# Up projections of latent attention moved beside the merge-logit pairs, block sums formed earlier, raw latents parked in DRAM

## The chip, the cores and the metric

The kernel runs on one core of one Trainium2 chip. The metric is device time of one execution in microseconds (us). Five engines work beside each other, each with its own instruction queue that is worked off in order: TensorE (PE, matmuls, with its weight loads PEld), VectorE (DVE), ScalarE (ACT), GpSimd (POOL, here mostly an issuer of DMAs) and SyncE (SP, issues DMAs). All PE results land in PSUM banks, from which ACT and DVE take them.

## The reference, cut to what matters

Two layers, each on a stream of 1024 tokens and 1024 channels:

```python
def hybrid_layer(x, c_act, cos, sin, ...):
    u = x * (1.0 + scale[:, None, :]) + shift[:, None, :]
    proj = jnp.einsum("bsd,dp->bsp", u, w_in)
    a_in, a_gate, b_in, b_gate, q_lat, kv_lat, k_rope, c_gate, merge_logits = jnp.split(proj, split_pts, axis=-1)
    ...                     # A: GLU, causal conv of 31 taps, LayerNorm, swish; B: conv of 3 taps, gated
    q = jnp.einsum("bsr,rk->bsk", rms_norm(q_lat, q_norm_g), w_uq).reshape(b, s, MLA_HEADS, QK_NOPE + QK_ROPE)
    kv = jnp.einsum("bsr,rk->bsk", rms_norm(kv_lat, kv_norm_g), w_ukv).reshape(b, s, MLA_HEADS, QK_NOPE + V_HEAD)
    ...                     # rotary parts, causal attention of 8 heads, times SiLU(c_gate)
    m = g_a * y_a + g_b * y_b + g_c * y_c          # g = sigmoid(merge_logits)
    out = jnp.einsum("bsd,de->bse", m, w_o)
    return layer_norm(DEEPNORM_ALPHA * x + gate[:, None, :] * out, ln_g, ln_b)
```

## The kernel before, in words

Everything is channel-major: a tile is 128 channels by 512 tokens, and the tokens are two halves, h = 0 and 1. Each float32 operand is split into a rounded high part and the rest (`split`, lines 124 to 133: a copy on ACT, L129, then a subtraction on DVE, L130), and each product is three matmuls (high by high, high by low, low by high). So every weight block of 128x512 costs an ACT and a DVE instruction before PE can use it.

A layer is a list of jobs in the order in which they are to run; `run` issues them one after the other and loads the weights of jobs up to four units ahead. The program is then ordered within each engine's queue by a scheduler, so that an instruction may move a little from the place of its job. `weave` and `blend` merge two lists, by number of jobs and by stated cost of PE work.

- **The head of a layer.** For each half the two kv and three q latents are products of u with W_in (`latps`, L186 to L188, four jobs of six matmuls each) and the rotary key (`krps`). Each raw latent is copied to a tile `lat` of the tag `w` (six buffers of 128x512 for the whole kernel), and its squares are summed. `rstd_jobs` makes the RMS factor from that (a sum over channels on PE, `qv`, then eight short DVE instructions `rs` and a row that PE spreads, `rstd`). `norm` scales the raw latents and splits them into pairs `latn`.
- **The up projections** (`up_jobs`): `kps` (k without rotation), `vps` (values), `qps`, and `x1ps` with `x2ps` (rotary q). Each result is split into a tile of the tag `sp` (two buffers) and stored to DRAM by a DMA on POOL's queue.
- **The block sums** (`s_job`, four of them): from the four x tiles of a channel pair (two channel blocks by two token halves) it makes the sums S1 to S4. Four x tiles (`xu`, tag `w`) are loaded on SP's queue and scaled on ACT, and four subtractions or additions and four splits follow on DVE and ACT.
- **The pairs** (`pair_jobs`): two channel blocks of a projection by all 1024 tokens are made with seven block products instead of eight (Strassen's scheme in Winograd's form), from X11, S1, S2, X12, S3, S4, X22. A pair is 84 matmuls at L295. The sums for all channels must be there before its second product is done. Twelve pairs make the merge logits (`lgps`), then come A (`aps`), C's gate (`cgps`), B (`xgps`, `bgps`) and A's gate (`agps`). The 31-tap convolution of each A pair is 31 DVE instructions on 128x1024 (L721, L725), woven beside the logit pairs that follow (`fill`).

Before the change one layer runs: the head of h = 0 with the u tiles (layer 1: the LayerNorm of the layer before) beside it; then `mix`, the head of h = 1 blended with the up projections of h = 0, with the four `s_job`s put in at four places; then two logit pairs blended with the up projections of h = 1; then four times an A pair and three further pairs with its convolution; then the B pairs with the LayerNorm of A (`lna`), and A's gates.

Of the kernel before, what the change touches and what calls it, by code (L numbers as in the profile page):

```python
# [16 lines left out]
P = 128  # L17
T = 512
# [28 lines left out]
def homes(a, b):  # L47
# [7 lines left out]
    "kvn0": ["u23", "u22"], "qn0": ["u11", "u7", "u19"], "kvn1": ["ab", "ab"], "qn1": ["c0", "c1", "c2"],  # L55
# [45 lines left out]
class Trunk:  # L101
# [391 lines left out]
    def s_job(self, l, i):  # L493

        nc = self.nc
        x11, x12, x21, x22 = (self.affine(l, h, 2 * i + e, act=True) for h in range(2) for e in range(2))
        tt = nc.vector.tensor_tensor
        tt(x11, x11, x21, op=ALU.subtract)
        self.factor(l, "S3", x11)
        tt(x21, x21, x22, op=ALU.add)  # L500
        self.factor(l, "S1", x21)
        tt(x22, x22, x11, op=ALU.subtract)
        self.factor(l, "S2", x22)
        tt(x12, x12, x22, op=ALU.subtract)
        self.factor(l, "S4", x12)
# [41 lines left out]
    def rms_jobs(self, l, h, which, tags=None):  # L547
        nc = self.nc
        st = {"t": []}
        n, ch, g = (3, CH_Q, V_QG) if which == "q" else (2, CH_KV, V_KG)  # L550

        def chunk(j):
            def fn(ps):
# [8 lines left out]
                st["t"].append(t)  # L562
            return self.in_chunk(l, h, ch + j, fn, "latps", tags[j] if tags else "pj")

        def norm(_):
            r = st["r"]
            res = []
            for j, t in enumerate(st["t"]):
                v = self.vec[l][:, g + j:g + j + 1]
                nc.vector.scalar_tensor_tensor(t[:, :T], t[:, :T], v, r, op0=ALU.mult, op1=ALU.mult)  # L570
                p = self.pair(f"{which}n{h}", "latn")
                self.split(p, t[:, :T])
                res.append(p)
            self.state[which + "n", l, h] = res
        return [chunk(j) for j in range(n)], self.rstd_jobs(st, 128 * n, "rms", ("tp", "tp")) + [([], norm)]
# [578 lines left out]
    def head(self, l, h, tags=(None, None)):  # L1154
# [3 lines left out]
        lat = kv[0] + kv[1] + weave(q[0] + q[1] + q[2], kvn, 2, 10) + self.krope_job(l, h)  # L1158
        ukv, uq = self.up_jobs(l, h)
        return lat, weave(ukv, qn, 0, 3) + uq  # L1160
# [15 lines left out]
    def build(self):  # L1176
        self.setup_early()
        jobs, first, adas = [], [], []
        for l in range(L):
# [29 lines left out]
            lat1, up1 = self.head(l, 1)  # L1209
            sums = [([], lambda _, l=l, i=i: self.s_job(l, i)) for i in range(4)]  # L1210
            n = len(up0)
            mix = blend(lat1, up0)
            where = [i for i, j in enumerate(mix) if any(j is u for u in up0)]
            for at, sj in sorted(zip((6, 12, where[4], where[-1]), sums), key=lambda p: -p[0]):
                mix.insert(at + 1, sj)
            jobs += mix

            lg = [self.logit_pair(l, n, 2 * i) for n in range(3) for i in range(4)]
            body = blend(lg[0] + lg[1], up1)
            convs = [self.conv_jobs(l, j) for j in range(4)]  # L1220
            fill = [lg[2] + lg[3] + lg[4], lg[5] + lg[6] + lg[7], lg[8] + lg[9] + lg[10],
# [156 lines left out]
```

## Time and profile before

| | before |
|---|---|
| median of 3 runs | 2282.19 us (2275.01 to 2285.17) |
| profiled execution, its own time | 2280.31 us |
| its span in the profile | 2278.1 us |
| busy: PE, DVE, ACT, POOL | 94%, 80%, 50%, 10% of the span |
| mean granted TensorE clock | 0.976 of full speed |

The busy share is an average over stages. PE is nearly always busy from the A pairs on, and has its holes in the heads of the two layers and around the attention. A matmul that runs at the lower clock counts as busy too, for longer.

### The profile page before, as it was taken

Reading aid. Unit: us, or ns where it says so; the run is one execution under the profiler, and the core shown is the slowest. Engines: PE = TensorE matmul, PEld = TensorE weight load, DVE = VectorE, ACT = ScalarE, POOL = GpSimd, SP = SyncE. Lnnn points to the kernel's source line nnn. Section 1 sums busy time; section 2 is a strip of 40 time slices with the busy share of each in tenths; the row PEclk is TensorE's granted clock in tenths of the full one; section 3 lists DMA queues with packets and bytes.
Section 4 is the critical chain, followed back from the end, with each engine's and each line's share of the span. In section 5 each row is a group of like instructions: output and inputs, shape, how many; then the busy total and the mean of one; then the engine's idle time right before and its main releaser. Section 6 shows DMA issues by size and latency. Waiting matters only on the chain.

```text
span 2278.1 us, 29704 instructions
## 1 busy us (share of the span) xinstructions
PE 2148.4 (94%) x10097; PEld 1724.4 (76%) x10097; DVE 1815.8 (80%) x2910; ACT 1139.8 (50%) x2072; POOL 226.4 (10%) x467
## 2 busy tenths in 40 slices
PE   8788999999999999988997799999999999999896
PEld 7566888888778778866775578888887778888686
DVE  4677789989887678777867868889898867867786
ACT  2665333333443656656447553334334447666753
POOL 4001000000001321101001010000000023211000
PEclk9989999999999999998999899999999999999998
DMA  7467322223222996665537572222222259755442
GB/s 262 151 202 225 120 105 105 101 100 108 77 82 89 231 243 183 183 178 184 187 108 208 188 216 82 90 102 93 84 92 70 65 155 226 207 135 149 156 158 65
DMA packets 181606, 328.28 MB, mean 144 GB/s; under 512 B 22096, under 2 KB 46928, under 8 KB 181456
## 3 DMA queue, kind: packets, MB, share of 16 engines
q1 hardware_dynamic: 122256, 214.30, 30.1%
q0 software_dynamic: 45376, 86.93, 14.8%
q10 hardware_dynamic: 13824, 25.17, 2.9%
q8 instruction: 79, 1.29, 0.2%
q14 instruction: 71, 0.58, 0.1%
HBM read 249.96 MB, written 76.35 MB: 143 GB/s over the span
## 4 chain that ended last, share of the span: by engine, by line
PE 78%; issue 9%; DMA 5%; DVE 5%; ACT 3%; POOL 0%; SPq 0%; POOLq 0%; DVEq 0%; ACTq 0%
PE lgps L295 21%; PE bgps L295 7%; PE xgps L295 7%; PE aps L295 7%; PE cgps L295 3%; PE yps L186 3%; PE agps L295 3%; PE yps L187 3%; PE yps L188 3%; PE avps L943 3%; PE tps L927 3%; PE ops L186 2%; PE ops L187 2%; PE ops L188 2%; PE score L903 1%
## 5 line engine op out<-in xcount | busy, mean ns | idle before, releaser
L295 PE MATMUL lgps<-u,wsplit 128*128 128x512 f32 x2016 | 477.4, 395 | 2.0 <-ACT u L129 0.8
L129 ACT CAST wsplit<-wraw 128x512 fp32r<-128x512 f32 (+1 forms) x524 | 318.4, 615 | 304.9 <-DVE wraw L220 45.6
L295 PEld LDWEIGHTS lgps<-u,wsplit 128*128 128x128 f32 x2016 | 377.3, 188 | 96.3 <-ACT u L129 1.8
L130 DVE TENSOR_TENSOR wsplit<-wraw,wsplit 128x512 fp32r<-128x512 f32 (+1 forms) x524 | 354.3, 681 | 69.8 <-ACT wsplit L129 67.8
L725 DVE SCALAR_TENSOR_TENSOR cacc<-abuf,vec,cacc 128x1024 f32<-128x1024 f32 x240 | 307.4, 1281 | 0.5
L295 PE MATMUL bgps<-u,wsplit 128*128 128x512 f32 x672 | 160.5, 397 | 0.0
L295 PE MATMUL xgps<-u,wsplit 128*128 128x512 f32 x672 | 159.9, 397 | 0.0
L295 PE MATMUL aps<-u,wsplit 128*128 128x512 f32 x672 | 158.3, 395 | 0.0
L295 PEld LDWEIGHTS xgps<-u,wsplit 128*128 128x128 f32 x672 | 126.3, 188 | 31.3 <-issue 1.0
L295 PEld LDWEIGHTS bgps<-u,wsplit 128*128 128x128 f32 x672 | 125.8, 188 | 31.7 <-issue 1.8
L295 PEld LDWEIGHTS aps<-u,wsplit 128*128 128x128 f32 x672 | 126.0, 188 | 30.8
L130 DVE TENSOR_TENSOR pt<-tps,pt 128x512 fp32r<-128x512 f32 (+1 forms) x160 | 100.9, 634 | 35.5 <-ACT pt L129 34.3
L129 ACT CAST pt<-tps 128x512 fp32r<-128x512 f32 (+1 forms) x160 | 85.7, 540 | 74.2 <-PE tps L927 71.4
L943 PE MATMUL avps<-pt,Vh 128*128 128x256 f32 x640 | 120.0, 302 | 2.3 <-ACT pt L129 2.0
L908 DVE TENSOR_REDUCE nm<-score 128x1 f32<-128x384 f32 (+7 forms) x128 | 95.8, 751 | 28.4 <-PE score L906 27.8
L186 PE MATMUL yps<-y,wsplit 128*128 128x512 f32 x256 | 107.0, 421 | 9.8 <-DVE mf L1014 5.9
L910 ACT ACTIVATE prob<-score,nm 128x384 f32<-128x384 f32 (+7 forms) x128 | 94.3, 740 | 43.2 <-PE tps L927 25.0
L186 PE MATMUL ops<-m,wsplit 128*128 128x512 f32 (+1 forms) x320 | 115.3, 360 | 0.0
L188 PE MATMUL ops<-m,wsplit 128*128 128x512 f32 (+1 forms) x320 | 113.1, 353 | 0.0
L187 PE MATMUL ops<-m,wsplit 128*128 128x512 f32 (+1 forms) x320 | 112.9, 353 | 0.0
L927 PE MATMUL tps<-cs,prob 128*128 128x128 f32 x576 | 92.6, 278 | 15.6 <-DVE pt L130 15.2
L943 PEld LDWEIGHTS avps<-pt,Vh 128*128 128x128 f32 x640 | 95.2, 194 | 14.5 <-ACT pt L129 7.8
(316 smaller groups left out, 4262.6 us busy)
## 6 DMA issues: line engine op xcount, KB each, us to landing
wraw<-in_win SPq DMA_DIRECT2D x264, 256.0 KB, 2.6
wraw<-in_wout SPq DMA_DIRECT2D x96, 256.0 KB, 3.0
mt<-tD SPq DMA_DIRECT2D x96, 256.0 KB, 4.4
adaraw<-in_wada SPq DMA_DIRECT2D x64, 256.0 KB, 3.3
wraw<-in_wo SPq DMA_DIRECT2D x64, 256.0 KB, 3.1
tD<-mt ACTq DMA_DIRECT2D x48, 256.0 KB, 2.0
Kh<-knD POOLq DMA_DIRECT2D x48, 256.0 KB, 5.0
Vh<-vD POOLq DMA_DIRECT2D x48, 256.0 KB, 5.2
```

The lines of the kernel that those rows point to most:

```text
L129: nc.scalar.copy(dst[:, 0], src)
L130: nc.vector.tensor_tensor(dst[:, 1], src, dst[:, 0].bitcast(F32), op=ALU.subtract)
L186: mm(ps, w[:, 0, c], x[k][:, 0, cols], start=k == 0, stop=False)
L187: mm(ps, w[:, 0, c], x[k][:, 1, cols], start=False, stop=False)
L188: mm(ps, w[:, 1, c], x[k][:, 0, cols], start=False, stop=k == n - 1)
L295: mm(ps, w[:, a, c], x[:, e], start=n < 2 and k == 0 and i == 0, stop=k == 3 and i == 2, skip_group_check=True)
L725: nc.vector.scalar_tensor_tensor(acc, a[:, k:k + S], w, acc, op0=ALU.mult, op1=ALU.add)
L903: mm(o, q[0:96, 0, qc], k[0:96, 0, :w], start=True, stop=False)
L908: nc.vector.tensor_reduce(nm[:, 0:1], sp[:, :nk], axis=AX.X, op=ALU.max, negate=True)
L910: nc.scalar.activation(p[:, :nk], sp[:, :nk], AF.Exp, bias=nm[:, 0:1], accum_out=nm[:, 1:2])
L927: nc.tensor.transpose(tp[:, c:c + P], st["p", hd, 2 * half + b][:, (2 * kp + k) * P:(2 * kp + k + 1) * P], self.ident)
L943: mm(av[:, half * 256:(half + 1) * 256], v[:, 2 * kp + k], pt[:, w, (1 - k) * 256:(2 - k) * 256], start=kp == 0 and k == 0 and w == 0, sto ...
```

## The change

The jobs are put in another order, and some get another home for their tiles; what is computed stays the same. Of the raw latents only the kv latents of h = 0 stay in their `w` tiles. The other eight of a layer are written to DRAM tensors `latq...` and `latkv...` on POOL's queue and read back on SP's queue when `norm` wants them, which is now one job per latent. The `mix` stage holds only the head of h = 1 and the four block sums. The up projections of h = 0 stand beside three logit pairs, those of h = 1 beside the next three, together with the first convolution. The first B pair moves into the last `fill`. `s_job` loads its third and fourth x tile later.

```diff
-    "kvn0": ["u23", "u22"], "qn0": ["u11", "u7", "u19"], "kvn1": ["ab", "ab"], "qn1": ["c0", "c1", "c2"],
+    "kvn0": ["ab", "ab"], "qn0": ["c0", "c1", "c2"], "kvn1": ["c3", "ab"], "qn1": ["c1", "c2", "c3"],
...
     def s_job(self, l, i):
-        x11, x12, x21, x22 = (self.affine(l, h, 2 * i + e, act=True) for h in range(2) for e in range(2))
         tt = nc.vector.tensor_tensor
+        x11, x21 = (self.affine(l, h, 2 * i, act=True) for h in range(2))
         tt(x11, x11, x21, op=ALU.subtract)
         self.factor(l, "S3", x11)
+        x22 = self.affine(l, 1, 2 * i + 1, act=True)
         tt(x21, x21, x22, op=ALU.add)
         self.factor(l, "S1", x21)
         tt(x22, x22, x11, op=ALU.subtract)
         self.factor(l, "S2", x22)
+        x12 = self.affine(l, 0, 2 * i + 1, act=True)
         tt(x12, x12, x22, op=ALU.subtract)
         self.factor(l, "S4", x12)
...
     def rms_jobs(self, l, h, which, tags=None):
+        keep = (which, h) == ("kv", 0)
...
-                st["t"].append(t)
+                if keep:
+                    st["t"].append(t)
+                else:
+                    d = self.pd.tile([P, T], F32, name=f"lat{which}{l}{h}{j}")
+                    nc.gpsimd.dma_start(d, t)
+                    st["t"].append(d)
...
-        def norm(_):
-            r = st["r"]
-            res = []
-            for j, t in enumerate(st["t"]):
+        def norm(j):
+            def fn(_):
+                t = st["t"][j]
+                if not keep:
+                    t = self.t2("w", "latb")
+                    nc.sync.dma_start(t, st["t"][j])
                 v = self.vec[l][:, g + j:g + j + 1]
-                nc.vector.scalar_tensor_tensor(t[:, :T], t[:, :T], v, r, op0=ALU.mult, op1=ALU.mult)
+                nc.vector.scalar_tensor_tensor(t, t, v, st["r"], op0=ALU.mult, op1=ALU.mult)
...
-        lat = kv[0] + kv[1] + weave(q[0] + q[1] + q[2], kvn, 2, 10) + self.krope_job(l, h)
-        return lat, weave(ukv, qn, 0, 3) + uq
+        if h == 0:
+            lat = kv[0] + kv[1] + weave(q[0] + q[1] + q[2], kvn, 2, 11) + kr[:1] + qn[:1] + kr[1:]
+            return lat, weave(ukv, qn[1:], 0, 2) + uq
+        lat = kv[0] + kv[1] + q[0] + kvn[:1] + q[1] + q[2] + kr[:1] + qn[:1] + kr[1:]
+        return lat, kvn[1:], ukv, qn[1:], uq
...
-            lat1, up1 = self.head(l, 1)
+            lat1, kvn1, ukv1, qn1, uq1 = self.head(l, 1)
             sums = [([], lambda _, l=l, i=i: self.s_job(l, i)) for i in range(4)]
-            n = len(up0)
-            mix = blend(lat1, up0)
-            where = [i for i, j in enumerate(mix) if any(j is u for u in up0)]
-            for at, sj in sorted(zip((6, 12, where[4], where[-1]), sums), key=lambda p: -p[0]):
-                mix.insert(at + 1, sj)
-            jobs += mix
+            jobs += weave(lat1, sums, 3, len(lat1) - 2)
...
-            body = blend(lg[0] + lg[1], up1)
+            body = blend(lg[0] + lg[1] + lg[2], up0[:-1] + kvn1 + up0[-1:])
...
-            fill = [lg[2] + lg[3] + lg[4], lg[5] + lg[6] + lg[7], lg[8] + lg[9] + lg[10],
-                    lg[11] + self.cg_pair(l, 0) + self.cg_pair(l, 2)]
+            fill = [blend(lg[3] + lg[4] + lg[5], weave(ukv1, qn1, 1, 3) + uq1), lg[6] + lg[7] + lg[8], lg[9] + lg[10] + lg[11],
+                    self.cg_pair(l, 0) + self.cg_pair(l, 2)]
+            b = [self.b_pairs(l, j) for j in range(4)]
+            fill[3] += b[0]
...
-            tail = [x for j in range(4) for x in self.b_pairs(l, j)]
+            tail = [x for j in range(1, 4) for x in b[j]]
...
-            body += weave(tail, lna, 20, len(tail) - 14)
+            body += weave(tail, lna, 6, len(tail) - 10)
```

On PE, at the end of the latents of h = 1 in layer 0, the order before puts an up projection of h = 0 (`vps`) between two latents (`latps`, the number behind a name tells tiles apart; u_605 and u_699 are the last two u tiles of h = 1):

```order
L186 MATMUL latps_712<-u_605,wsplit_466 128x512
...
L188 MATMUL latps_712<-u_699,wsplit_550 128x512
L670 MATMUL vps_787<-wsplit_658,latn_578 128x512
...
L670 MATMUL vps_800<-wsplit_658,latn_578 128x512
...
L670 MATMUL vps_813<-wsplit_658,latn_578 128x512
...
L670 MATMUL vps_826<-wsplit_658,latn_578 128x512
...
L543 MATMUL rstd_934<-rsrow_772,onesr_70 128x512
L186 MATMUL latps_887<-u_385,wsplit_709 128x512
```

In the changed kernel the latents of h = 1 run through to the rotary key, and the first logit pair (`lgps`) follows; u_825, u_910, u_1002 and u_1069 are the S2 sums of the four `s_job`s:

```order
L188 MATMUL latps_977<-u_721,wsplit_842 128x512
...
L616 MATMUL krps_1042<-u_721,wsplit_922 128x512 x2
L295 MATMUL lgps_1126<-u_164,wsplit_933 128x512 x3
...
L307 MATMUL kps_1138<-latn_570,wsplit_970 128x512
...
L295 MATMUL lgps_1126<-u_285,wsplit_933 128x512 x3
...
L295 MATMUL lgps_1168<-u_825,wsplit_1039 128x512 x3
L295 MATMUL lgps_1168<-u_910,wsplit_1039 128x512 x3
L545 MATMUL rstd_1198<-rsrow_688,onesr_70 128x512
L295 MATMUL lgps_1168<-u_1002,wsplit_1039 128x512 x3
L295 MATMUL lgps_1168<-u_1069,wsplit_1039 128x512 x3
```

What moved: all four values blocks, and the other up projections with them, left the stretch of the latents, and the logit pair now comes directly behind it, with the last S2 sum as the first thing that it can lack.

On DVE, in the same stretch of layer 0, the first `s_job` stood before among the splits of the up projections and of the latents:

```order
L130 TENSOR_TENSOR latn_1042<-lat_597,latn_1042 128x512
L679 TENSOR_TENSOR vsp_833<-vps_826,vsp_833 128x4x64
L498 TENSOR_TENSOR xu_849<-xu_849,xu_855 128x512
L679 TENSOR_TENSOR vsp_833<-vps_826,vsp_833 128x4x64
L130 TENSOR_TENSOR wsplit_919<-wraw_917,wsplit_919 128x512
L130 TENSOR_TENSOR u_862<-xu_849,u_862 128x512
L500 TENSOR_TENSOR xu_855<-xu_855,xu_858 128x512
L561 TENSOR_TENSOR sq_847<-sq_847,sq_914 128x512
L502 TENSOR_TENSOR xu_858<-xu_858,xu_849 128x512
```

In the changed kernel the `s_job`s follow each other, here the second, between the steps of an RMS factor (`rs`):

```order
L498 TENSOR_TENSOR xu_892<-xu_892,xu_895 128x512
L513 CAST rs_881<-rs_881 128x128
L501 TENSOR_TENSOR xu_895<-xu_895,xu_902 128x512
L514 SCALAR_TENSOR_TENSOR rs_881<-rs_881,cs_127 128x128
L503 TENSOR_TENSOR xu_902<-xu_902,xu_892 128x512
L515 TENSOR_TENSOR rsrow_888<-rs_881,cs_127 128x512
L130 TENSOR_TENSOR u_899<-xu_892,u_899 128x512
L130 TENSOR_TENSOR u_906<-xu_895,u_906 128x512
L130 TENSOR_TENSOR u_910<-xu_902,u_910 128x512
L506 TENSOR_TENSOR xu_913<-xu_913,xu_902 128x512
```

What moved: the splits of the up projections and the scaling of the q latents are gone from this stretch of DVE's queue, and the sums stand close together.

## Rows read from the trace of the kernel before

**Rows 1.** Busy time by stretch (us, busy us with instructions, granted clock, DMA share)

```profile
core 0: us, PE busy (x) PEld busy (x) DVE busy (x) ACT busy (x) POOL busy (x), PEclk, DMA share, GB/s
75.50:130.10 54.60, 41.99 (x162) 29.22 (x161) 41.31 (x76) 36.58 (x68) 6.25 (x9) 0.94 0.71 201
130.10:239.60 109.50, 94.69 (x394) 72.32 (x393) 82.78 (x144) 61.13 (x111) 12.89 (x23) 0.94 0.68 206
250.00:515.00 265.00, 265.00 (x1142) 213.69 (x1141) 241.82 (x298) 102.97 (x179) 0.35 (x3) 1.00 0.29 101
1196.50:1222.30 25.80, 16.53 (x64) 11.36 (x62) 20.23 (x35) 21.63 (x36) 5.38 (x10) 0.80 0.40 134
1222.30:1254.00 31.70, 27.78 (x121) 20.63 (x120) 23.85 (x46) 21.88 (x42) 5.71 (x8) 1.00 1.00 271
1254.00:1360.00 106.00, 90.34 (x371) 69.22 (x370) 80.11 (x139) 57.98 (x105) 12.36 (x22) 0.94 0.67 203
```

**Rows 2.** Short matmuls of the RMS sums, 75.5 to 239.6 us (busy us, mean ns)

```profile
L528 PE MATMUL qv<-sq,ones 128*32 128x128 f32 x24 | 1.3, 285 | 0.0
```

**Rows 3.** What TensorE waited for, 60 to 240 us (total us, times, longest)

```profile
PE x2ps L307 <- ACT sq L557: 6.4, 1, 6.4
PE vps L670 <- ACT sq L557: 5.1, 1, 5.1
```

**Rows 4.** Timeline of TensorE around 105 us (start, duration, [idle before, releaser])

```profile
102.22 0.79 PE L670 MATMUL vps<-wsplit,latn 128*128 128x512 f32 x1 [5.08 <-ACT sq L557]
...
104.09 0.63 PE L671 MATMUL vps<-wsplit,latn 128*128 128x512 f32 x1
104.52 0.63 PE L672 MATMUL vps<-wsplit,latn 128*128 128x512 f32 x1
...
106.65 0.58 PE L671 MATMUL vps<-wsplit,latn 128*128 128x512 f32 x1
```

**Rows 5.** Timeline of VectorE in the heads of both layers

```profile
92.35 0.67 DVE L130 TENSOR_TENSOR u<-xu,u 128x512 fp32r<-128x512 f32 x1
...
95.62 0.93 DVE L534 RECIPROCAL rs<-rs 128x128 f32<-128x128 f32 x1
...
97.82 0.27 DVE L536 SCALAR_TENSOR_TENSOR rs<-rs 128x128 f32<-128x128 f32 x1
...
1221.66 0.62 DVE L130 TENSOR_TENSOR u<-xu,u 128x512 fp32r<-128x512 f32 x1
...
1252.52 0.69 DVE L500 TENSOR_TENSOR xu<-xu 128x512 f32<-128x512 f32 x1
1253.12 0.69 DVE L130 TENSOR_TENSOR u<-xu,u 128x512 fp32r<-128x512 f32 x1
```

**Rows 6.** Timeline of ScalarE, scaling and splitting of u tiles, layer 0

```profile
88.97 1.63 ACT L462 ACTIVATE xu<-xu,ada 128x512 f32<-128x512 f32 x2
90.51 1.12 ACT L129 CAST u<-xu 128x512 fp32r<-128x512 f32 x2
```

**Rows 7.** Timeline of VectorE beside the convolution, from 318 us

```profile
318.93 0.69 DVE L130 TENSOR_TENSOR wsplit<-wraw,wsplit 128x512 fp32r<-128x512 f32 x1
319.53 1.28 DVE L725 SCALAR_TENSOR_TENSOR cacc<-abuf,vec,cacc 128x1024 f32<-128x1024 f32 x1
320.72 0.69 DVE L220 TENSOR_TENSOR wraw<-wraw 128x512 f32<-128x512 f32 x1
```

**Rows 8.** DMA issues of the whole span (count, size, median us to landing)

```profile
xu<-in_xT SPq DMA_DIRECT2D x32, 256.0 KB, 3.6
tD<-mt ACTq DMA_DIRECT2D x48, 256.0 KB, 2.0
cgD<-gt POOLq DMA_DIRECT2D x16, 256.0 KB, 2.3
```

**Rows 9.** Timeline of TensorE in the logit pairs, 186 to 195 us

```profile
186.13 0.47 PE L670 MATMUL vps<-wsplit,latn 128*128 128x512 f32 x1 [2.14 <-DVE vsp L679]
...
190.03 0.47 PE L670 MATMUL vps<-wsplit,latn 128*128 128x512 f32 x1 [2.27 <-DVE vsp L679]
```

More of the change, by code (lines that the diff above doesn't have):

```diff
@@ L561, in fn @@
                     nc.vector.tensor_tensor(st["ss"], st["ss"], sq, op=ALU.add)
-                st["t"].append(t)
-            return self.in_chunk(l, h, ch + j, fn, "latps", tags[j] if tags else "pj")
-        def norm(_):
-            r = st["r"]
-            res = []
-            for j, t in enumerate(st["t"]):
+                if keep:
[4 more added lines that the diff above has]
+                    st["t"].append(d)
+            return self.in_chunk(l, h, ch + j, fn, "latps", tags[j] if tags else "pj")
+        def norm(j):
[4 more added lines that the diff above has]
+                    nc.sync.dma_start(t, st["t"][j])
                 v = self.vec[l][:, g + j:g + j + 1]
-                nc.vector.scalar_tensor_tensor(t[:, :T], t[:, :T], v, r, op0=ALU.mult, op1=ALU.mult)
+                nc.vector.scalar_tensor_tensor(t, t, v, st["r"], op0=ALU.mult, op1=ALU.mult)
                 p = self.pair(f"{which}n{h}", "latn")
[L572 to L575, printed above, removed]
+                self.split(p, t)
+                self.state.setdefault((which + "n", l, h), []).append(p)
+            return ([], fn)
+        return ([chunk(j) for j in range(n)],
+                self.rstd_jobs(st, 128 * n, "rms", ("tp", "tp")) + [norm(j) for j in range(n)])
     def krope_job(self, l, h):
@@ L1157, in head @@
         q, qn = self.rms_jobs(l, h, "q", tags[1])
-        lat = kv[0] + kv[1] + weave(q[0] + q[1] + q[2], kvn, 2, 10) + self.krope_job(l, h)
         ukv, uq = self.up_jobs(l, h)
-        return lat, weave(ukv, qn, 0, 3) + uq
+        kr = self.krope_job(l, h)
+        if h == 0:
[3 more added lines that the diff above has]
+        return lat, kvn[1:], ukv, qn[1:], uq
     def phase(self, l, n, jobs):
```

## The prediction

> **What bounds the kernel now.** By the table above TensorE is at work for 94% of the span, so a change of order can only win back what PE loses: holes, and matmuls at the lower clock, which count as busy. I therefore read busy time by stretch first. Beside the logit and A pairs PE is full: 1142 matmuls in 265.00 us, 0.232 us each, with DVE at 241.82 of 265 us (91%) [rows 1]. That is the pace of an undisturbed PE. In the heads of the two layers it is not kept. From the rotary key of h = 0 to the first A pair, layer 0 takes 54.60 + 109.50 = 164.1 us for 162 + 394 = 556 matmuls, and layer 1 takes 25.80 + 31.70 + 106.00 = 163.5 us for 64 + 121 + 371 = 556 [rows 1]. In each layer 24 of them are short ones with 1.3 us in all [rows 2]. At full pace either stretch needs 532 x 0.232 + 1.3 = 124.7 us, so PE loses 39.4 us in layer 0 and 38.8 us in layer 1, together 78.2 us.
>
> Next, what PE waited for. Its longest waits in layer 0 are of an up projection, `x2ps` 6.4 us and `vps` 5.1 us, each for `sq` on ACT, that is for the PSUM bank of a latent that ACT had not yet emptied [rows 3]. In the timeline the 5.08 us wait is followed by matmuls 0.43 us apart (104.09 to 104.52), up to about 106.65, against 0.232 at full clock [rows 4]: one long wait costs some 2 us more, the granted clock being at its lower level of 1.2 GHz. Beside the logit pairs, too, `vps` waits 2.14 and 2.27 us for its split, both for DVE's `vsp` [rows 9]. So latents, up projections and block sums contend for ACT, DVE and the buffers behind them, while in 250 to 515 us nothing stops PE.
>
> **The change part by part.**
>
> *What stays.* The matmuls and the DVE and ACT arithmetic are the same in number; only 16 stores and 16 loads of 256 KB are new. From the first A pair on PE is full before the change, so the sum is made from the two heads and from what the moved work does in its new place.
>
> *The head without up projections.* In the changed order PE runs the latents of h = 1 and the rotary key, then the first block product of a logit pair, six matmuls of `kps`, and half of the S2 product; then it needs the S2 sum of the fourth `s_job` (u_1069 in the order). Up to there, from the key of h = 0 on, it has 178 full matmuls and the 24 short ones: 178 x 0.232 + 1.3 = 42.6 us. The same count holds in layer 1. The other side is DVE. The last u tile of h = 1 is split at 92.35 us in layer 0 and at 1221.66 us in layer 1 [rows 5]; the work ahead of it hardly changes, so I keep both times. DVE's queue in the changed kernel then holds up to that sum: in layer 0 55 instructions of 512 columns, 11 short ones and a reciprocal; in layer 1 50, 6 and one. Back to back they follow each other at 0.60 us (1252.52 to 1253.12), the short ones at about 0.3, the reciprocal at about 0.9 [rows 5]. Layer 0: 33.0 + 3.3 + 0.9 = 37.2 us, so the sum is there at 92.95 + 37.2 = 130.1 us. Layer 1: 30.0 + 1.8 + 0.9 = 32.7 us, thus 1222.3 + 32.7 = 1255.0 us. ACT has 59 instructions in the same stretch of layer 0, 16 scalings at 0.77 and 43 others at about 0.51 [rows 6], 34 us: DVE ends last. PE has then lost 130.1 - 75.5 - 42.6 = 12.0 us in layer 0 and 1255.0 - 1196.5 - 42.6 = 15.9 us in layer 1, where the wait for the LayerNorm ahead of the u tiles is in it before and after. Together 27.9 us: if nothing else were lost, the gain would be 78.2 - 27.9 = 50.3 us.
>
> *What is given back.* (a) The `s_job`s are fed through the six `w` buffers: 16 x tiles and 5 latents in that stretch. An x tile lives for its load, 3.6 us [rows 8], the scaling, and some six DVE instructions with queueing, about 11 us; a latent about 3.5 us (two ACT instructions, then a store like `cgD`, 2.3 us [rows 8]). (16 x 11 + 5 x 3.5) / 6 = 32 us, as long as DVE's own queue, so now and then a load comes too late. Bounds per layer: 0, and 4 x (3.6 + 0.8) = 17.6 us, each `s_job` waiting for one load in full. I take 4 us per layer, since half of the tiles can be loaded ahead. (b) One wait of some 10 us per layer drops the clock: 2 us each [rows 4]. (c) The up projections beside the pairs: `vps` loses 4.4 us there before [rows 9]; three of its four blocks stand close together again, while the fourth and all others have pair matmuls between them. I take 3 us for each of the two sets of a layer, bounds 0 and 8. All three, for both layers: 8 + 4 + 12 = 24 us.
>
> *Edits costed at nothing.* The convolution beside the second set: the first A pair and its fill hold 439 full matmuls, 101.9 us, and on DVE 85 instructions at 0.60, 31 of the convolution at 1.2 (319.53 to 320.72 [rows 7]; the first one a little shorter) and 14 smaller ones at 0.3 to 0.5, 93 us. That is 91% of PE's time, as it was; the cover is thinner by nothing, but what PE waits for now stands behind steps of 1.2 us (a rival below). From the fourth A pair to the last B pair DVE has some 196 us beside 214 us of PE, again 91%. The latents' loads come back on SP's queue among weights that are fetched four units ahead, 11 us at four times 12 matmuls; a load of 3.6 us is covered by that, and where it is not, the norm of the q latents is late, and `qps` with it. The stores stand on POOL's queue ahead of the rotary key's and the up projections' stores, and nothing but the six buffers waits for them.
>
> A 256 KB store from POOL's queue lands in 2.3 us in the median of a span with DVE busy for 80% of it, one from ACT's in 2.0 us [rows 8], so I cost it at nothing beyond the life of the `w` tile. The Trainium skill's page "SBUF — State Buffer", section "Who interferes with whom", speaks against the choice of that queue: GpSimd writes the descriptors of its DMAs itself and is locked out of a port while VectorE runs an instruction in a two-port mode. By that rule a store could lie still for one DVE instruction, at most 1.3 us, and the sum would be at most 8 x 1.3 / 6 = 1.7 us worse per layer; the rows show 0.3 us.
>
> **Sum.** 50.3 - 24 = 26 us less than the profiled execution's own time: 2280.3 - 26 = 2254 us. That execution lies 2 us below the median of the three runs, which is within their spread.
>
> **The rivals.**
>
> *A. The block sums starve.* Each `s_job` waits in full for a load because its buffers come free only when the one before is through. Price: 17.6 instead of 4 us per layer, 27 us in all at most; with some 18 of them the time is 2272 us. For it: 21 tiles go through six buffers. Against it: SP issues the first x tiles of the next `s_job` well ahead. The Trainium skill's page "Perfetto Trace Analysis", section "Identifying Performance Opportunities", says that the same gap again and again on the engine that should be full can mean that there are too few buffers for the next tile; by that rule the six `w` buffers would go on deciding.
>
> *B. The loss only moves.* What PE lost in the head it loses in the first logit pairs, waiting for up projections whose splits go through the two `sp` buffers. Price: about 26 us, thus 2280 us. For it: `vps` waits there already [rows 9]. Against it: six logit pairs instead of two now lie beside the two sets.
>
> *C. Slower: the convolution's DVE queue stops PE.* In the first fill 14 PSUM tiles of up projections must be emptied through a queue with 31 steps of 1.2 us. If each holds PE up for one such step and its own split, 1.8 us, that is 25 us per layer instead of 3: 44 us, and 2254 + 44 = 2298 us. The gain is gone from 1.15 us per tile on. Against it: 9% of free DVE time in that fill, and two or three banks, with pair matmuls between.
>
> **How the numbers follow.** Chances: 0.65 for the forecast (2238 to 2267 us, from its bounds), 0.18 for A, 0.10 for B, 0.07 for C. A is split by the bound of 0.5% (11.4 us, about what a measurement of this kernel can tell from no change): up to 2270.8 us it is faster, 0.12 of 0.18. So faster 0.77, same 0.06 + 0.10 = 0.16, slower 0.07. The range should leave out C, most of B, and as much on the low side: 2238 to 2275 us. The low end is the gain without (a) and with half of (b) and (c), 50.3 - 8 = 42 us.
>
> **What the profile after would show.** Right: between 75 and 130 us PE runs latents without a `vps` among them; one wait of 5 to 12 us per layer of `lgps` for u on DVE or ACT, near 120 and 1250 us; the first A pair's 439 matmuls in 102 to 106 us. The two heads' lost time, counted as above, falls from 78 to some 52 us. Wrong: several waits of `lgps` or idle ACT before `xu`, released by DMA (A); `vps` or `kps` waits beside lgps adding up to over 15 us per layer (B); PE below 95% beside the first convolution with DVE full (C). A later u tile of h = 1 than 92 or 1222 us would shift every number of the head.

## The result, and the profile after

The changed kernel takes 2255.88 us (median of 4 runs, 2255.18 to 2257.43), the kernel before 2282.82 us (median of 4, 2275.01 to 2285.17): a ratio of 0.989, interval 0.9875 to 0.9904. The forecast was 2254 us, range 2238 to 2275. Two repeats gave 0.9876 and 0.9894 (intervals in the table below). The profiled execution took 2257.4 us, its span is 2254.8.

Busy time by stretch after, with the columns of [rows 1]: from the rotary key of h = 0 to the first S2 product of a logit pair, on to the first A pair, and the first A pair with most of its fill; then the same three stretches of layer 1.

```profile
73.30:129.40 56.10, 44.45 (x196) 32.85 (x194) 50.02 (x91) 47.02 (x83) 4.35 (x8) 0.97 0.63 202
129.40:212.50 83.10, 80.93 (x339) 64.23 (x340) 58.59 (x101) 41.96 (x77) 9.61 (x16) 0.98 0.72 209
212.50:315.00 102.50, 100.27 (x429) 80.22 (x428) 86.82 (x119) 44.21 (x83) 8.51 (x14) 1.00 0.61 181
1180.00:1241.60 61.60, 45.30 (x196) 33.65 (x194) 51.41 (x92) 51.57 (x89) 8.12 (x15) 0.86 0.53 179
1241.60:1325.60 84.00, 81.76 (x339) 64.43 (x340) 58.95 (x101) 41.95 (x78) 9.61 (x16) 0.98 0.70 207
1325.60:1426.00 100.40, 99.51 (x427) 79.67 (x426) 86.10 (x117) 44.27 (x84) 8.51 (x14) 1.00 0.59 175
```

The first and the fourth row hold 172 full matmuls and the 24 short ones, 41.2 us at the pace of the prediction, so PE loses 14.9 and 20.4 us. The second and fifth hold 339 (78.6 us) and lose 4.5 and 5.4 us; the third and sixth lose 102.5 - 99.5 = 3.0 and 100.4 - 99.1 = 1.3 us with a convolution beside them. From the key to the first A pair that is 45.2 us for both layers together, against 78.2 before and some 52 forecast. Here the stretch from the key to the first A pair is 139.2 us long in layer 0 and 145.6 in layer 1; it is 140.8 and 146.2 us in the repeat r2 and 142.2 and 147.7 in r3, so that some 2 and 5 us more are lost there. The first row also shows the two parts of such a loss: 56.10 - 44.45 = 11.7 us of holes, and 3.3 us by which PE's busy time is above that of the full pace; in layer 1 they are 16.3 and 4.1 us. The granted clock is 0.97 and 0.86 in these rows. Not all of the 3.3 us is the clock's, since the last matmul before each hole counts with its whole 0.39 us and not with the 0.232 us of the pace.

What TensorE waited for from 70 to 216 us (total, times, longest), for comparison with [rows 3]:

```profile
PE lgps L295 <- ACT lgps L260: 5.2, 2, 4.0
PE latps L186 <- DVE kra L599: 4.1, 1, 4.1
PE kps L307 <- ACT sq L560: 1.5, 1, 1.5
PE kps L307 <- DVE vsp L690: 0.9, 1, 0.9
```

and from 1178 to 1335 us in layer 1:

```profile
PE latps L186 <- ACT u L129: 7.4, 1, 7.4
PE lgps L295 <- ACT lgps L260: 6.8, 2, 5.3
PE kps L307 <- ACT sq L560: 3.5, 1, 3.5
```

The waits of `x2ps` and `vps` for a latent's bank are gone. In their place stands the wait of `lgps`, 4.0 us in layer 0 and 5.3 us in layer 1 at the longest, and it is not alone: in layer 0 `latps` waits for the bank that the rotary key holds until DVE's `kra`. The 7.4 us for the u tiles of the LayerNorm ahead in layer 1 are no part of the change: they stand in the trace of before with the same length.

The timeline of layer 0 shows, in this order, DVE's last u split of h = 1, ACT's copy that releases PE, PE's S2 product, and DVE's split of the last S2 sum.

```profile
89.39 0.63 DVE L130 TENSOR_TENSOR u<-xu,u 128x512 fp32r<-128x512 f32 x1
...
128.81 0.58 ACT L260 COPY lgps<-lgps 128x512 f32<-128x512 f32 x1
...
129.44 2.93 PE L295 MATMUL lgps<-u,wsplit 128*128 128x512 f32 x6 [4.03 <-ACT lgps L260]
...
130.15 0.69 DVE L130 TENSOR_TENSOR u<-xu,u 128x512 fp32r<-128x512 f32 x1
```

PE is let go at 129.44 us by ACT's copy, not by the S2 sum. That sum is split from 130.15 to 130.84 us, where the forecast had it at 130.1. The second half of the S2 product, which needs it, starts only at 132.59 us, the six matmuls of the first half having started 0.46 us apart (granted clock 0.64 from 129.4 to 133.9 us). So in this trace PE does not wait for the sum, though the copy lets it go only 1.4 us before the sum is there; e1 below shows what happens when the copy comes earlier. In layer 1 the copy lets PE go at 1241.65 us and the sum is there at 1243.39, 1.7 us later. DVE's and ACT's work between the last u split and the end of that split, in both layers:

```profile
90.02:130.84 40.82, 30.40 (x129) 22.85 (x130) 37.30 (x68) 33.37 (x58) 3.25 (x6) 0.94 0.63 200
1205.08:1243.39 38.31, 29.33 (x132) 22.31 (x131) 33.12 (x59) 33.44 (x58) 3.24 (x6) 0.89 0.63 206
```

DVE is busy for 37.30 of 40.82 us in layer 0, where 37.2 were forecast, and for 33.12 of 38.31 us in layer 1 (forecast 32.7). ACT has 33.37 and 33.44 us (34 were forecast for layer 0): in layer 1 it is as full as DVE.

The new transfers land, but for the reload of the kv latents, later than I had assumed (median us from issue to landing, as in [rows 8]):

```profile
latq<-lat POOLq DMA_DIRECT2D x12, 256.0 KB, 3.4
latb<-latq SPq DMA_DIRECT2D x12, 256.0 KB, 5.1
latkv<-lat POOLq DMA_DIRECT2D x4, 256.0 KB, 6.0
latb<-latkv SPq DMA_DIRECT2D x4, 256.0 KB, 3.4
```

A q latent needs 3.4 + 5.1 = 8.5 us through DRAM and a kv latent 6.0 + 3.4 = 9.4 us, where 2.3 + 3.6 = 5.9 us had been taken.

### The profile page after: what moved, and what is told of

Same layout as the page of the kernel before. It is cut to its first block, busy times and chain, and to the rows that moved or that the text cites. A ratio compares the mean times of both kernels' runs of the same rounds, so it can differ in the third digit from the quotient of the medians.

```text
span 2254.8 us, 29755 instructions
## 1 busy us (share of the span) xinstructions
PE 2139.8 (95%) x10097; PEld 1723.9 (76%) x10097; DVE 1810.3 (80%) x2910; ACT 1138.4 (50%) x2072; POOL 235.6 (10%) x483
## 4 chain that ended last, share of the span: by engine, by line
PE 75%; issue 11%; DMA 5%; DVE 4%; ACT 3%; POOL 1%; SPq 0%; POOLq 0%; DVEq 0%; ACTq 0%
PE lgps L295 19%; PE bgps L295 7%; PE xgps L295 7%; PE aps L295 7%; PE cgps L295 3%; PE agps L295 3%; PE yps L186 3%; PE yps L187 3%; PE yps L188 3%; PE avps L954 3%; PE tps L938 3%; PE ops L186 2%; PE score L914 2%; PE ops L187 2%; PE ops L188 2%
## 5 line engine op out<-in xcount | busy, mean ns | idle before, releaser
L295 PE MATMUL lgps<-u,wsplit 128*128 128x512 f32 x2016 | 483.9, 397 | 13.7 <-ACT lgps L260 12.0
L938 PE MATMUL tps<-cs,prob 128*128 128x128 f32 x576 | 93.1, 279 | 18.0 <-DVE pt L130 17.5
L954 PEld LDWEIGHTS avps<-pt,Vh 128*128 128x128 f32 x640 | 95.6, 195 | 14.2 <-ACT pt L129 7.4
```

The source lines that it names most:

```text
L295: mm(ps, w[:, a, c], x[:, e], start=n < 2 and k == 0 and i == 0, stop=k == 3 and i == 2, skip_group_check=True)
L938: nc.tensor.transpose(tp[:, c:c + P], st["p", hd, 2 * half + b][:, (2 * kp + k) * P:(2 * kp + k + 1) * P], self.ident)
L954: mm(av[:, half * 256:(half + 1) * 256], v[:, 2 * kp + k], pt[:, w, (1 - k) * 256:(2 - k) * 256], start=kp == 0 and k == 0 and w == 0, sto ...
```

## The experiments

Between the rotary key of h = 0 and the first score of the attention all these kernels run the same matmuls (the head, the logit, A, B and gate pairs), so that stretch and the attention and output stage behind it are listed apart, in us, for each profiled execution. The ratio is to runs of the kernel before beside it on the same chip, with its 95% interval. The runs r1 to r4 and e1 to e8 come from three chips: r1, r2, e1 and e2 from one, where the kernel before took 2281.7 us, e3 to e6 from a second (2283.7 us), and r3, r4, e7 and e8 from a third (2282.0 us). On the second the changed kernel itself did not run, so e3 to e6 are set against it by the ratio and by the stretches alone:

| kernel | time, median | ratio to before | key to score, layer 0, 1 | attention and output, layer 0, 1 |
|---|---|---|---|---|
| before | 2282.8 | | 680.4, 678.3 | 440.6, 403.2 |
| r1, before again | 2281.6 | 1.0002 (0.9989 to 1.0014) | 679.0, 677.6 | 440.4, 406.7 |
| after | 2255.9 | 0.989 (0.9875 to 0.9904) | 662.6, 665.6 | 444.1, 409.2 |
| r2, after again | 2253.3 | 0.9876 (0.9853 to 0.9899) | 664.4, 666.2 | 444.8, 407.2 |
| r3, after, third | 2257.0 | 0.9894 (0.9869 to 0.9919) | 664.7, 667.3 | 442.8, 406.1 |
| e1, X11 early | 2252.2 | 0.9874 (0.9852 to 0.9896) | 660.2, 665.2 | 443.2, 407.8 |
| r4, X11 early again | 2252.7 | 0.9867 (0.9846 to 0.9889) | 660.3, 665.2 | 445.0, 407.1 |
| e2, parking alone | 2304.2 | 1.0101 (1.0083 to 1.0119) | 685.8, 692.0 | 440.3, 408.1 |
| e3, key's bank by ACT | 2261.1 | 0.9905 (0.9886 to 0.9923) | 665.6, 669.0 | 437.7, 409.1 |
| e4, sums on GpSimd | 2270.0 | 0.9939 (0.9923 to 0.9955) | 670.6, 673.3 | 445.8, 406.4 |
| e5, five w buffers | 2267.7 | 0.9928 (0.9908 to 0.9948) | 666.9, 672.3 | 443.9, 407.6 |
| e6, old s_job | 2262.8 | 0.9909 (0.9893 to 0.9925) | 666.6, 671.9 | 439.1, 411.4 |
| e7, half the change | 2279.0 | 0.9986 (0.9968 to 1.0004) | 675.9, 680.3 | 442.3, 406.4 |
| e8, stores from ACT | 2263.9 | 0.9918 (0.9898 to 0.9938) | 667.9, 670.3 | 439.1, 407.2 |

**The two kernels again (r1, r2, r3).** Between the first two traces the stretch from key to score fell by 17.8 and 12.7 us and the part ahead of it by 2.3, yet the span by 23.3 only: the attention and output stages, whose instructions and order are the same, took 3.5 and 6.0 us longer. So I first looked at what repeats.

> The kernel before, unchanged, to see how far two traces of one program differ. In the trace of before the attention and output stages take 440.6 us in layer 0 (first score 756.0 to the rotary key of layer 1 at 1196.6) and 403.2 us in layer 1 (1874.9 to the end at 2278.1). The changed kernel, with the same instructions in the same order there, took 444.1 and 409.2 us, 9.5 us more in all. Theory 1, it is a property of the change (other places in DRAM, other arrival times): this run shows 440.6 and 403.2 again, each within 1 us. Theory 2, executions differ by that much: the two lengths lie anywhere between 440 and 445 and between 402 and 410, and the total moves with them (2275 to 2285 us).

> The changed kernel again, for the same question. Theory 1: 444.1 and 409.2 us in the two attention and output stages, each within 1 us, and a time of 2255 to 2258 us. Theory 2: the lengths differ from these by 2 us or more. The lost time of the heads should repeat either way: some 15 and 4.5 us in layer 0, 20 and 5.5 us in layer 1.

> The changed kernel a third time, as the yardstick for the runs beside it: 2250 to 2258 us, heads of 139 to 141 and 145 to 146 us. The attention stage of layer 0 took 437.7 to 445.8 us in kernels that differ from it in the head alone; if that is chance it may lie anywhere in between here.

The stretch from key to score repeats within 2.1 us, the difference between the kernels there being some 16 and 12 us. The attention stage of layer 0 took 440.3 to 440.6 us in the three traces with the old order and 442.8 to 444.8 in the three of the changed kernel, which looks like theory 1; but e3, e6 and e8, which differ from the changed kernel in the head alone, have 437.7, 439.1 and 439.1 us. In layer 1 the ranges overlap. So the stage moves by several us with small differences ahead of it. For both layers it takes 851.4 us on average in the three traces of the changed kernel, and 845.5 us in the two of the kernel before; but e2, with the old order, has 848.4 and e8, with the new one, 846.3. Whether the change costs this stage anything, and by what mechanism, stays open.

**Parking alone (e2).** The kernel before, with this and the loads at the norm:

```diff
-                st["t"].append(t)
+                if keep:
+                    st["t"].append(t)
+                else:
+                    d = self.pd.tile([P, T], F32, name=f"lat{which}{l}{h}{j}")
+                    nc.gpsimd.dma_start(d, t)
+                    st["t"].append(d)
```

> The kernel before, with its order of jobs, but the raw latents other than the first two are stored to DRAM and loaded back at their norm, as in the changed kernel. Theory 1 (the order makes the gain, parking only makes it possible): PE still waits for the PSUM banks of the latents behind ACT in the heads, which lose 72 to 86 us as before (78.2), and the time is 2278 to 2288 us. Theory 2 (the w buffers that the latents held were what delayed the heads): the heads lose 60 us or less, and the time is 2268 us or less.

It is slower than before, by 22 us, which neither theory had. What TensorE waited for, 70 to 245 us, and then 1188 to 1378 us in layer 1:

```profile
PE qps L307 <- ACT latn L129: 17.5, 2, 9.2
```

```profile
PE qps L307 <- ACT latn L129: 20.5, 2, 11.7
```

The long waits for `sq` are gone (0.9 us are left, in layer 1), but `qps` now waits for a normalised latent, twice and 17.5 us in all, in layer 1 20.5 us: 8.3 to 11.7 us each, about the round trip through DRAM. In the changed kernel `qps` waits 0.9 us for a latent at the longest (212 to 330 and 1325 to 1440 us): the norms stand many pair matmuls after the stores, and the round trip is hidden. In the old order parking costs some 22 us. So parking alone is not the gain; whether the `w` tiles that it frees would help if the round trip were hidden is not shown by this run.

**Half the change (e7).** The latents of h = 1 are parked and their up projections spread as in the changed kernel; those of h = 0 stay in the head:

```diff
-                keep = (which, h) == ("kv", 0)
+                keep = h == 0
...
-            jobs += weave(lat1, sums, 3, len(lat1) - 2)
+            mix = blend(lat1, up0)
+            where = [i for i, j in enumerate(mix) if any(j is u for u in up0)]
+            for at, sj in sorted(zip((6, 12, where[4], where[-1]), sums), key=lambda p: -p[0]):
+                mix.insert(at + 1, sj)
+            jobs += mix
...
-            body = blend(lg[0] + lg[1] + lg[2], up0[:-1] + kvn1 + up0[-1:])
+            body = blend(lg[0] + lg[1] + lg[2], kvn1)
```

> Half of the change: the up projections of h = 0 stay in the head among the latents of h = 1, in the old order and with the latents of h = 0 kept in SBUF; the latents of h = 1 are parked in DRAM and their up projections spread as in the changed kernel (beside the fourth to sixth logit pair of the list and the first convolution). From the first rotary key to the first A pair it has the same matmuls as the changed kernel. Theory 1 (the gain is that the up projections left the head, where they contend with the latents for ACT, DVE and PSUM banks): that stretch loses some 10 us more per layer than in the changed kernel (139 to 141 and 145 to 146 us), and the time is 2268 to 2282 us. Theory 2 (the second set's room beside six pairs and the w buffers freed by parking are what pays): the stretches stay within 4 us of the changed kernel's, 2250 to 2262 us.

Half the change gains nothing that can be told from zero. What TensorE waited for in the two heads (70 to 246 us, 1170 to 1365 us):

```profile
PE vps L681 <- DVE knope L130: 5.6, 2, 4.0
PE latps L186 <- DVE ra L665: 5.0, 1, 5.0
PE rstd L545 <- DVE rs L535: 3.1, 1, 3.1
PE latps L186 <- DVE vsp L690: 1.6, 1, 1.6
```

```profile
PE latps L186 <- DVE vsp L690: 5.5, 1, 5.5
PE latps L186 <- DVE ra L665: 4.7, 1, 4.7
PE rstd L545 <- DVE rs L535: 2.7, 1, 2.7
```

They are up projections and latents again, held by what DVE has to do with results of the up projections (the splits `knope` and `vsp`, the rotary step `ra`): 12.2 us in layer 0, and in layer 1 10.2 us and 2.0 more of `knope`. Theory 1 holds: against the mean of the three traces of the changed kernel the stretch is 12.0 us longer in layer 0 and 13.9 us in layer 1, together nearly the whole gain of 27.4 us. The long waits for `sq` do not come back, and yet nothing is gained: what the head loses does not hang on that one wait. With the up projections of h = 0, e7 also puts the `s_job`s back to their old places and keeps the q latents of h = 0 in their `w` tiles. How the gain divides among the three is not shown; no run moves the up projections or the block sums alone.

**The copy ahead of the fourth sum (e1, r4).** Does ACT's copy, which let PE go, cost the wait?

```diff
-            jobs += weave(lat1, sums, 3, len(lat1) - 2)
+            mix = weave(lat1, sums, 3, len(lat1) - 2)
+            at = [i for i, j in enumerate(mix) if j is sums[3]][0]
+            jobs += mix[:at] + lg[0][:2] + mix[at:]
```

(and those two jobs taken out of the body).

> The first block product of the first logit pair (X11, twelve matmuls) and ACT's copy behind it are put ahead of the fourth s_job in the program. The long wait before the S2 product (4.0 us in layer 0, 5.3 in layer 1) was released by that copy on ACT. Theory 1 (as predicted: DVE's S2 sum ends last, and the copy only came 1.4 us before it would have been lacked): PE runs the twelve matmuls earlier and waits for the S2 sum instead, which DVE gives at 130 to 131 us in layer 0 as now; at most 1.4 us per layer are won, 2253 to 2257 us. Theory 2 (the copy's place in ACT's queue holds PE up): the wait falls by 4 us or more per layer, 2245 to 2249 us.

> The first product ahead of the fourth s_job once more, beside the changed kernel on the same chip. Theory 1 (a wait for the sum takes the place of the wait for the copy): 0 to 3 us faster than the changed kernel beside it. Theory 2: 6 us or more faster.

The two traces are 3.7 and 1.2 us shorter per layer than the mean of the changed kernel, 4.9 us in all, and the time is 1.1 us less than beside it in the one case and 4.3 in the other. In layer 0 of e1 PE then waits for the sum itself:

```profile
132.42 0.69 DVE L130 TENSOR_TENSOR u<-xu,u 128x512 fp32r<-128x512 f32 x1
...
133.16 0.74 PE L295 MATMUL lgps<-u,wsplit 128*128 128x512 f32 x2 [0.59 <-DVE u L130]
```

The S2 split starts 132.42 - 75.7 = 56.7 us after the rotary key, 130.15 - 73.3 = 56.8 in the changed kernel. So with the copy out of the way the sum is what PE waits for, and it comes at the same time, as theory 1 has it. The long wait shrinks instead of moving whole: in layer 1 the gain of 1.2 us lies within the 1.4 expected, and within the spread of the changed kernel (665.6 to 667.3 us); in layer 0 3.7 us are above that and near what theory 2 had. In time the edit lies between the two theories, and the intervals of its ratios overlap those of the changed kernel.

**The rotary key's bank (e3).** ACT empties the whole PSUM tile, so that the 4.1 us wait for DVE's `kra` ends:

```diff
             nc.scalar.copy(b[0:64], ps[64:128])
-            nc.vector.tensor_tensor(a[0:64], ps[0:64], b[0:64], op=ALU.add)
+            nc.scalar.copy(a[0:64], ps[0:64])
+            nc.vector.tensor_tensor(a[0:64], a[0:64], b[0:64], op=ALU.add)
```

> One edit in the changed kernel: ACT copies the other half of the rotary key's PSUM tile too, so that its bank is free without DVE, whose queue held PE up for 4.1 us at 95 us of layer 0 (latps after kra). Theory 1 (DVE's queue up to the last S2 sum sets the end of the head, all PE waits ahead of it are inside that): the 4.1 us wait goes, the wait before the S2 product grows by about as much, the stretch from the first rotary key to the first A pair stays at 139 to 141 us, and the time at 2251 to 2257 us. Theory 2 (PE's waits add up, each is worth its own length): that stretch falls to 135 to 137 us, and the time by 4 us, to 2249 to 2252 us.

PE still waits 2.9 us, now for ACT, and DVE waits 3.5 us for scaled x tiles, 0.7 in the changed kernel (70 to 216 us on PE, 80 to 132 us on DVE):

```profile
PE latps L186 <- ACT kra L599: 2.9, 1, 2.9
```

```profile
DVE xu L498 <- ACT xu L462: 3.5, 2, 2.2
```

The stretch is 1.7 and 2.6 us longer than the changed kernel's mean, little more than its spread of 2.1 and 1.7 us, and the interval of the ratio overlaps the changed kernel's. The 4 us of theory 2 are not there; but as the edit took only 1.2 us off the wait, it is a weak test of what that wait is worth. In layer 0 the last S2 split starts 59.5 us after the rotary key, 56.8 in the changed kernel: with one more copy on ACT the sums come later there, which theory 1 did not have. In layer 1 the split does not move (63.3 us against 62.7 to 63.4).

**Sums on GpSimd (e4).** Two of the four subtractions of an `s_job`:

```diff
-        tt(x11, x11, x21, op=ALU.subtract)
+        nc.gpsimd.tensor_tensor(x11, x11, x21, op=ALU.subtract)
...
-        tt(x12, x12, x22, op=ALU.subtract)
+        nc.gpsimd.tensor_tensor(x12, x12, x22, op=ALU.subtract)
```

> In the changed kernel the subtractions for S3 and S4 (x11 - x21 and x12 - x22, two of the four per s_job) are done by GpSimd. Seven of the eight per layer stand on DVE ahead of the last S2 sum, 0.6 us each, 4.2 us; GpSimd's step is longer (0.74 us for 128x256 elsewhere in this trace, so an estimated 1.4 us here) and one of them lies in the last sum's own chain, 0.8 us. Theory 1 (DVE ends last): the last S2 split comes some 3 us earlier in each layer against the last u split of h = 1 (now 40.8 us after it in layer 0, 38.3 in layer 1), and the time falls by 4 to 7 us, to 2247 to 2250 us. Theory 2 (the loads through the six w buffers or ACT's casts pace the sums): the splits come as late as now, and the time is 2254 to 2260 us, later by the longer steps if anything.

It takes 2270.0 us, and the stretch is 6.7 and 6.9 us longer. GpSimd's steps (all of the span; busy us, mean ns):

```profile
L506 POOL TENSOR_TENSOR xu<-xu 128x512 f32<-128x512 f32 x8 | 16.1, 2018 | 11.1 <-DVE xu L503 6.4 <-ACT rs L534 2.1 <-DMA wraw<-in_wukv 2.1
L498 POOL TENSOR_TENSOR xu<-xu 128x512 f32<-128x512 f32 x8 | 12.4, 1548 | 27.1 <-ACT xu L462 27.1
```

1.55 and 2.02 us, not 1.4. They also hold up DVE; the timeline of e4, and behind it the same cast in the changed kernel:

```profile
114.66 1.78 POOL L498 TENSOR_TENSOR xu<-xu 128x512 f32<-128x512 f32 x1 [3.44 <-ACT xu L462]
...
115.19 1.32 DVE L513 CAST rs<-rs 128x128 fp32r<-128x128 f32 x1
```

```profile
110.84 0.22 DVE L513 CAST rs<-rs 128x128 fp32r<-128x128 f32 x1
```

The cast starts at 115.19 us and ends at 116.51, just after GpSimd's step (116.44), and takes 1.32 instead of 0.22 us. In layer 0 the split of the last S2 sum, which reads two SBUF tiles, takes 1.50 us beside GpSimd's L506, 0.69 in the changed kernel. The Trainium skill's page "SBUF — State Buffer", section "Who interferes with whom", says that DVE and GpSimd share a pair of ports under an exclusive lock, that a cast on DVE can enter a mode which takes it, and that a DVE instruction with two SBUF inputs contends with a GpSimd one that reads SBUF; the cast and the split agree. Both theories fail: that split starts 137.70 - 75.8 = 61.9 us after the rotary key, 56.8 in the changed kernel, so seven instructions less on DVE are outweighed by longer steps in the sums' own chain.

**The w buffers (e5, e6).** One buffer less, and the old order of loads:

```diff
-        bufs = dict(tab=1, wr=6, ws=6, tt=1, sp=2, ab=2, w=6, x=2, n=5, sm=8, acc=1)
+        bufs = dict(tab=1, wr=6, ws=6, tt=1, sp=2, ab=2, w=5, x=2, n=5, sm=8, acc=1)
```

```diff
-        x11, x21 = (self.affine(l, h, 2 * i, act=True) for h in range(2))
+        x11, x12, x21, x22 = (self.affine(l, h, 2 * i + e, act=True) for h in range(2) for e in range(2))
...
-        x22 = self.affine(l, 1, 2 * i + 1, act=True)
...
-        x12 = self.affine(l, 0, 2 * i + 1, act=True)
```

> The changed kernel with five w buffers instead of six. Theory 1 (term a: the x tiles and latents need (16 x 11 + 5 x 3.5) / 6 = 32 us of buffer time, about as much as DVE's queue, and starve now and then): with five it is 39 us, the last S2 sum comes 4 to 7 us later per layer, ACT waits longer for the DMA of xu, and the heads lose 8 to 14 us more; the buffers are used in the later stages too, so the total says less than the heads. Theory 2 (loads are well ahead, the buffers don't pace the sums): the heads stay within 2 us of 139 to 141 and 145 to 146 us.

> The changed kernel with the old s_job: all four x tiles are loaded and scaled first. Theory 1 (the buffers are short): x12, which is needed last, now holds a buffer for some 5 us longer and keeps the next s_job's tiles out; the last S2 sum comes 1 to 5 us later per layer, 2256 to 2264 us. Theory 2 (the order of the loads is worth nothing): within 2 us of the changed kernel in the heads, 2251 to 2257 us.

Five buffers cost 3.0 and 5.9 us in the stretch, the old order of loads 2.7 and 5.5 us. In layer 1 of e5 the waits of `kps` grow, for `sq` from 3.5 us and for `vsp` from under 1 us in the changed kernel (1178 to 1335 us):

```profile
PE kps L307 <- ACT sq L560: 5.8, 1, 5.8
PE kps L307 <- DVE vsp L690: 5.6, 1, 5.6
```

In layer 0 the last S2 split starts 59.4 us (e5) and 59.2 us (e6) after the rotary key, 56.8 to 57.4 in the three traces of the changed kernel. Theory 1 holds for e6; for e5 it holds in what the heads lose, 9.7 us more from the key to the first A pair in both layers together, but the sum of layer 0 comes 2.4 us later where 4 to 7 were expected. So the number of buffers that term (a) counts is a real limit: taking one away costs 8.9 us in the two stretches, and the old order of loads 8.2. Seven were not tried.

**The queue of the stores (e8).**

```diff
-                    nc.gpsimd.dma_start(d, t)
+                    nc.scalar.dma_start(d, t)
```

> The changed kernel with the stores of the raw latents issued from ACT's queue instead of GpSimd's. In the changed kernel these stores landed 3.4 us (q) and 6.0 us (kv) after issue, against 2.3 us for cgD from the same queue. Theory 1 (the Trainium skill, page SBUF - State Buffer, section Who interferes with whom: GpSimd's descriptors wait for VectorE): the stores land in 2.0 to 2.5 us, the w tiles come back earlier, and the heads are up to 1.7 us shorter per layer. Theory 2 (ACT's queue is as tight as DVE's, one more instruction on it cost some 3 us per layer): the heads get 1 to 3 us longer. Theory 3: the landing time is that of the DMA engines, which are crowded there, it stays at 3 to 6 us, and the heads stay within 1 us.

The landing times of these stores over the whole span:

```profile
latq<-lat ACTq DMA_DIRECT2D x12, 256.0 KB, 3.5
latkv<-lat ACTq DMA_DIRECT2D x4, 256.0 KB, 4.1
```

The q stores land in 3.5 us, as from GpSimd's queue (3.4), the kv stores in 4.1 instead of 6.0, and the stretch is 4.0 and 3.9 us longer than the changed kernel's mean: theory 2 in direction, with more than it had expected, and theory 3 for the landing of the twelve q stores. By the rule of the Trainium skill's page that theory 1 names the stores would have landed sooner; that holds at most for the four kv stores. Where the 4 us arise is only in part shown: in layer 0 the last S2 split starts 56.0 us after the rotary key, not later than in the changed kernel (56.8), and PE waits 3.7 us for `rs` and 3.2 us for `vsp`; in layer 1 it starts 66.0 us after the key against 62.7.

## Why the prediction was right

**The heads.** The sum rested on the lost time falling from 78 to some 52 us; it fell to 45.2, or 49.5 with the two second sets beside the first convolution, which the 52 contained (some 2 and 5 us more in r2 and r3). PE lost 14.9 and 20.4 us up to the S2 product, where 12.0 + 4 + 2 = 18 and 15.9 + 4 + 2 = 21.9 stood. That the head of h = 1 has to be cleared, and that parking alone or the spread of the second set does not make the gain, is shown by e2 and e7: parking in the old order costs 22 us, and with the set of h = 0 left in the head nothing is gained.

**DVE's queue to the last S2 sum** was counted right (37.30 and 33.12 us busy, forecast 37.2 and 32.7), and e1 shows PE waiting for that sum once the copy is out of the way. Other edits bear out that the sum sets the end of the head in layer 0: where its split starts later, the stretch grew with it, by 1.7 us for 59.5 us after the key (e3), 3.0 for 59.4 (e5), 2.7 for 59.2 (e6) and 6.7 for 61.9 (e4), against 56.8 to 57.4 in the three traces of the changed kernel; e8 is the exception. In the changed kernel itself the step "DVE ends last" is not exact: ACT's copy let PE go, 1.4 and 1.7 us before the sum was there. The sign that the prediction named, one wait of 5 to 12 us for u, came as a wait for that copy, of 4.0 and 5.3 us. And the hit at 130.1 us is in part luck: I kept the last u split at 92.35 us, and it came at 89.39. Of these 3.0 us 2.2 belong to the whole head, whose key came at 73.3 and not at 75.5; they and the 0.7 that are left nearly cancel the 3.5 us that DVE stood idle, which were term (a) and not in the 130.1.

**(a)** DVE stood idle for 3.5 us in layer 0 and 5.2 us in layer 1 in that stretch; 4 was the term. I had put it to loads that come late. The waits that end these holes name ACT instead; the longest in layer 1:

```profile
DVE xu L498 <- ACT xu L462: 1.9, 1, 1.9
DVE wsplit L130 <- ACT wsplit L129: 1.4, 2, 0.9
DVE u L130 <- ACT u L129: 0.7, 2, 0.4
```

ACT itself waited eight times for an x tile in layer 0 (80 to 132 us), 5.5 us with none over 1.3, and e5 and e6 show that buffers and load order count. The prediction had counted 34 us for ACT and then left it out, because DVE had more; but ACT, with 33.4 us in the same stretch, feeds the sums: e8, which adds to ACT's queue, lost time, and e3 too, if hardly more than the traces differ.

**(b)** was 2 us per layer. PE's busy time is 3.3 and 4.1 us above the full pace, behind several waits and not one of 10 us; but adding (b) to a head that DVE ends counts it twice. Up to the end of the S2 split PE lost 130.84 - 73.3 - 42.6 = 14.9 us in layer 0, and that is 12.0 + 3.5 of DVE's idle time + 0.1 of its work - 0.7 for the earlier u split; in layer 1 20.8 = 15.9 + 5.2 + 0.4 - 0.7. No (b) is left in either: slower matmuls ahead of the sum only fill time in which PE would have waited. The sums of the prediction were 3.1 and 1.1 us too long there, 2 us of it by (b). **(c)** was 3 us per set, 12 in all; 4.5, 3.0, 5.4 and 1.3 us make 14.2. Rival C is refuted by the third and sixth row of the first table: beside the convolution 3.0 and 1.3 us are lost, not 25. Of rival A the mechanism exists at five buffers and with the old order of loads. Rival B, of which over 15 us of waits per layer were to be the sign, is refuted: no wait of `vps` is left, and `kps` waits 2.4 us in all in layer 0 (0.9 of it for `vsp`) and some 4 us in layer 1.

**Edits costed at nothing.** The parked latents' round trip of 8.5 to 9.4 us was taken as 5.9; it stays hidden in the changed kernel, but for 0.9 us at the longest. What I did not forecast is the attention stage, some 6 us longer in these traces. The heads and pairs won 27.4 us (means of two and three traces: 1357.7 and 1330.3 us for both layers) where 26 were forecast, and the attention stages took 5.9 back. The mean spans differ by 22.3 us (2277.1 and 2254.8), the medians by 26.9, 28.4 and 25.0 us, since the two profiled executions of before lie below the medians of their series, by 2.5 and 3.3 us, and two of the three of the changed kernel above theirs, by 1.6 and 4.2. That the forecast hits within 2 us is therefore closer than its terms deserve: (b) was counted twice, and the attention stage was not looked at. Its largest term, the head that is left when the up projections are gone, is what the runs bear out.

## What to carry to other kernels

Work that shares the emptying engines and PSUM banks with a stretch that is bound by them belongs beside a stretch in which TensorE alone is full; room for that can be bought by parking data in DRAM, but only if the reload stands a full round trip, here 9 us, ahead of its use. Count the queue of the busiest engine, and beside it that of the engine that feeds it: here, with 37.3 and 33.4 us in the same stretch, one more copy on the feeding engine won nothing (e3). Measure a gain by the stage in which it arises, since equal stages behind it can differ by several us.

## What was not expected of the hardware

An elementwise subtraction of 128x512 took GpSimd 1.55 to 2.02 us beside a busy VectorE, against 0.69 us on VectorE, and a VectorE cast of 128x128 that met one took 1.32 us instead of 0.22. A store of 256 KB from the same queue landed in 2.3 us in one stage and in 3.4 and 6.0 us in another, and the same stage of the same instructions took 437.7 to 445.8 us.
